# Two projections' weights: split into two parts once, the parts kept in a DRAM scratch and fetched for the later segments

## The chip, the core and the metric

The kernel runs on one core of one Trainium2 chip. The metric is the device time of that core for one execution, in microseconds (us). The engines are named as the profile names them: PE is TensorE (PEld are its weight loads), DVE is VectorE, ACT is ScalarE, POOL is GpSimd and SP is SyncE, whose queue issues most of the transfers.

## The reference: what is computed

One layer of a streaming encoder for 1024 frames of a new stream and 64 frames of a running one, model width 1024, all in float32:

```python
h = _rms_norm(x, norm1_g)
parts = jnp.split(h @ w_in, np.cumsum(IN_SIZES)[:-1].tolist(), axis=-1)   # w_in: 1024 x 3080
o_a, s_new, conv_new = _gdn_mixer(...)      # gated delta rule, 4 heads, blocks of 64
o_b, v_rows = _gmlp_mixer(...)              # spatial gating over chunks of 128
o_c = _swa_prompt(...)  or  _swa_sample(...)   # sliding-window attention with sinks
x = x + jnp.concatenate([o_a, o_b, o_c], axis=-1) @ w_out                 # w_out: 1024 x 1024
h = _rms_norm(x, norm2_g)
x = x + (jax.nn.silu(h @ w_gate) * (h @ w_up)) @ w_down                   # 1024 x 2816 and back
```

## The kernel before

**Products in two parts.** A float32 operand is written as h + l: h is the value rounded to the matmul format `fp32r`, l the rest. A product is three matmuls (h·h, h·l, l·h). ACT makes h by a copy (`acopy`, line 86), DVE makes l by a subtraction (`tt`, line 92).

**Segments.** The 1088 frames go through the input projection in three segments (`SEGS`): frames 0 to 383, 384 to 767, and 768 to 1023 with the 64 sample frames. Each segment multiplies by the whole of `w_in`. The matrix is cut into 24 pieces of about 512 KB, in this order: two of `g0`, two of `sq`, twelve of the convolution channels (`p0`, `p1`), two of `u`, two of `vm`, four of `z`. The output projection takes `w_out` in four pieces per half of its columns; its first half of columns is used twice, for frames 0 to 767 (`wo_plan[0]`) and at the end for the rest (`wo_plan[2]`), its second half once (`wo_plan[1]`). So there are 84 pieces, 72 of them from `w_in`.

**The class `Weights`.** `load` starts the transfer of one raw piece into one of three buffers `wr` (line 120, SP's queue), always up to three pieces ahead. `split` turns the raw piece into its parts `hw` and `lw`: two ACT copies and two DVE subtractions (four each for the first two pieces). The parts lie in one of three slots of `wts`; a fourth slot (`he`, `le`) is there during the output projection alone. The matmuls read the parts. When the last one of a piece has read them, its slot goes to the piece three places later.

**What PE does meanwhile.** The matmuls of the projections (`mm<-xh,hw` and the like: 24 for a group, in a bank `mm`) alternate with short ones of the mixers (all `ax<-...`): the delta rule, the attention, the gating, which ACT and DVE feed. `g0`, `sq` and `vm` go by frames: a group takes both pieces of such a pair, 12 matmuls on the first and 12 on the second, so both stay in their slots for three groups. The others go by channels: one group to a piece.

**After the mixers.** `out_proj` handles the first six blocks of 128 frames, `out_last(1, ...)` and then `out_last(0, wo_plan[2], o)` the last three. While these run, DVE and ACT also prepare the feed-forward stage: sums and splits of the normalised input (`x<-x,x`, `x_sums`), the same for its first weights (`w<-w,w`, `w_sums`, `w_split`). When the last group of a block is done, DVE adds it to the residual (`last_y`), ACT and POOL compute the norm (`norm2`), PE transposes the result (line 275), and the feed-forward matmuls (line 1462) go on with it.

**The order of instructions** on each engine is set by a list scheduler when the program is built: it orders them by a cost model of its own, so an instruction removed on one engine can move others. On the chip each engine, and each queue, works through its own list in order. From the feed-forward stage's last weights on the order is written by hand.

Of the kernel before, what the change touches and what calls it, by code (L numbers as in the profile page):

```python
# [7 lines left out]
F32 = mybir.dt.float32  # L8
# [4 lines left out]
ALU = mybir.AluOpType  # L13
# [40 lines left out]
def hybrid_step(ctx, tc, x_prompt, x_sample, cache_k, cache_v, st_gdn, st_conv, norm1_g, w_in, conv_w, a_log,  # L54
# [3 lines left out]
    V, A, G, T, SP = nc.vector, nc.scalar, nc.gpsimd, nc.tensor, nc.sync  # L58
# [17 lines left out]
    def sb(p, shape, tag, dt=F32, bufs=None):  # L76
        return p.tile(shape, dt, tag=tag, name=tag, bufs=bufs)
# [7 lines left out]
    def acopy(out, in_, scale=1.0):  # L85
        return A.activation(out=out, in_=in_, func=AF.Copy, scale=scale)  # L86
# [4 lines left out]
    def tt(out, in0, in1, op):  # L91
        return V.tensor_tensor(out=out, in0=in0, in1=in1, op=op)  # L92
# [8 lines left out]
    class Weights:  # L101
        def __init__(self):
            self.src, self.free, self.fresh, self.raw, self.got = [], [], [], {}, {}
            self.nd = self.ns = self.want = 0
            self.retired = None

        def slots(self, p, n, tag):
            self.free += [(p, f"{tag}{i}") for i in range(n)]

        def add(self, a, b, parts):  # L110
            self.src.append((a, b, parts))
            return len(self.src) - 1

        def load(self):
            i = self.nd
            a, b, parts = self.src[i]
            r = sb(wp, [128, 1056], "wr", bufs=3)
            v = r[:, :a * b].rearrange("p (a b) -> p a b", a=a)
            for lo, hi, k0, k1, c0, c1, s in parts:
                SP.dma_start(out=v[lo:hi, k0:k1, c0:c1], in_=s)  # L120
            self.raw[i] = r
            self.nd += 1

        def split(self):
            i = self.ns
            while self.nd <= i:
                self.load()
            a, b, _ = self.src[i]
            r, n = self.raw.pop(i), a * b
            p, t = self.free.pop(0)  # L130
            h = sb(p, [128, 1056], "h" + t, F32R)
            l = sb(p, [128, 1056], "l" + t, F32R)
            m = b if i < 2 else n // 2
            for c in range(0, n, m):
                acopy(h[:, c:c + m], r[:, c:c + m])
                tt(l[:, c:c + m], r[:, c:c + m], h[:, c:c + m].bitcast(F32), ALU.subtract)
            self.got[i] = ((p, t), h[:, :n].rearrange("p (a b) -> p a b", a=a),
                           l[:, :n].rearrange("p (a b) -> p a b", a=a))
            self.ns += 1
# [38 lines left out]
    W = Weights()  # L178
# [3 lines left out]
    plan = []  # L182
    for s in range(3):
        d = {}
# [17 lines left out]
    wo_plan = []  # L202
    for h in (0, 1, 0):
        c0 = 512 * h
        ids = []
        for kk in range(3):
            s_ = w_out[0, kk * 256:kk * 256 + 256, c0:c0 + 512].rearrange("(k p) c -> p k c", p=128)
            ids.append(W.add(2, 512, [(0, 128, 0, 2, 0, 512, s_)]))
        s_ = []
        for kv in range(2):  # L210
            s_.append((64 * kv, 64 * kv + 64, 0, 2, 0, 512,
                       w_out[0, 768 + 128 * kv:896 + 128 * kv, c0:c0 + 512].rearrange("(g d) c -> d g c", d=64)))
        ids.append(W.add(2, 512, s_))
        wo_plan.append(ids)

    wg_ = w_gate[0].rearrange("(k p) c -> p k c", p=128)
    wu_ = w_up[0].rearrange("(k p) c -> p k c", p=128)
# [1118 lines left out]
    def x_sums(c):  # L1336
        R = raw[c]
        B11, B21, B12, B22 = R[0, 0], R[1, 0], R[0, 1], R[1, 1]

        def split(n, v, late=0):  # L1340
            h, lo = x_tile(c, late=late > 0), x_tile(c, late=late > 1)
            acopy(h, v)
            tt(lo, v, h.bitcast(F32), ALU.subtract)
            X[c][n] = (h, lo)

        T1 = x_tile(c, F32)
        tt(T1, B12, B11, ALU.subtract)
        split("B11", B11)
        yield
        T2 = x_tile(c, F32)  # L1350
        tt(T2, B22, T1, ALU.subtract)
        split("T1", T1)
        yield
        T4 = x_tile(c, F32)
        tt(T4, B21, T2, ALU.subtract)
        split("T2", T2)
        yield
        split("B21", B21)
        yield
        tt(B12, B22, B12, ALU.subtract)  # L1360
        split("T3", B12, 1)
        yield
        split("B22", B22, 1)
        yield
        split("T4", T4, 2)
# [86 lines left out]
    later = []  # L1452
# [202 lines left out]
    def d_ops(kp):  # L1655
# [34 lines left out]
        def sub(n):  # L1690
# [11 lines left out]
            for j in range(2):  # L1702
# [3 lines left out]
                (("d", 0, diff, ("T1", "T2", "T3", "T4")), ("v", 0, lambda n: diff(n, V), ("T1", "T2", "T3", "T4")), ("r", 1, rnd, ("R1", "R2", "T13", "T24")),  # L1706
                 ("s", 1, sub, ("R1", "R2", "T13", "T24"))) for n in ns} | {
                     "L1": (1, lambda: load(0)), "L2": (1, lambda: load(1))}

    ORDER0 = ((-6, "aL1 aL2"), (0, "bL1 bL2 aT1d"), (1, "aT3d aR1r"), (2, "aT2d aR1s"), (3, "aT4d aT13r"),  # L1710
# [122 lines left out]
    for b, p, n, f in work:  # L1833
        k = b if p == "s" else (b, p, n)
# [23 lines left out]
    for u in range(22):  # L1858
# [6 lines left out]
        for i, s in enumerate(steps):  # L1865
# [7 lines left out]
            if i >= 7 or u not in (0, 21):  # L1873
                n = i - 7 if u in (0, 21) else i // 2
# [85 lines left out]
```

## Time and profile before

| | |
|---|---|
| median of 3 runs | 1357.01 us (1356.85 to 1358.77) |
| the profiled execution's own time | 1357.18 us |
| its span, first to last instruction | 1355.2 us |
| first segment, second, third (by the first `g0` matmul) | from 14.2, 168.8 and 341.8 us |
| output projection | 497.6 to about 621 us |
| feed-forward stage, gate and up | about 621 to 1085 us |
| feed-forward stage, down | to the end |

The profile shows one execution. Its page lists busy times, groups of instructions by line and tile, and the transfers; the trace behind it gives each instruction's start and duration, and what ended an engine's idle time. In a row of the timeline stand start, duration, engine, line, operation, tiles (out<-in), shape and count, and in brackets the idle time before it and who ended it. Matmuls overlap, so the time that one takes is the distance to the next start. A table of windows gives busy time and number of instructions for each engine in each stretch, then the granted clock of PE (1.00 is full), the busy share of the 16 DMA engines and their rate.

### The profile page before, as it was taken

The page shows a single profiled execution, that of the slowest core. Times are in us where ns is not written, and L with a number is a line of the kernel's source. Part 1 is how long each engine was busy: PE and PEld are TensorE (multiplying, and loading weights), DVE is VectorE, ACT ScalarE, POOL GpSimd, SP SyncE. Part 2 cuts the span into 40 slices and gives each one's busy share as a digit, 9 for nine tenths or more (in the row PEclk, how much of TensorE's full clock was granted, in tenths as well). Part 3 has the DMA queues.
Part 4 walks back from the last instruction along what each step waited for, and adds up shares of the span by engine and source line. Part 5 has one row for each costly group of instructions (what it writes and reads, how often), then busy time and mean ns, then how long its engine had stood idle before and what let it go on. Part 6 is the DMA issues. An engine that isn't in the chain of part 4 may idle for free.

```text
span 1355.2 us, 26537 instructions
## 1 busy us (share of the span) xinstructions
PE 1316.4 (97%) x9922; PEld 1170.9 (86%) x9922; DVE 986.2 (73%) x2286; ACT 683.4 (50%) x1725; POOL 183.4 (14%) x250
## 2 busy tenths in 40 slices
PE   6999999999999999998999999999999988999997
PEld 6988888888878887787999999999999976777784
DVE  6887877867788785588866777667776687767764
ACT  7677376674667653556555554455544532222202
POOL 3100130101121210100000000000000343232104
PEclk9999999999999999998999999999999999999999
DMA  8422342223233161322434544355443499666645
GB/s 259 122 79 64 82 116 78 79 64 80 70 93 94 49 214 51 121 78 86 126 120 152 176 136 124 111 156 175 132 124 112 159 320 335 223 225 238 215 142 198
DMA packets 205011, 189.00 MB, mean 139 GB/s; under 512 B 13931, under 2 KB 174160, under 8 KB 204882
## 3 DMA queue, kind: packets, MB, share of 16 engines
q1 hardware_dynamic: 196690, 174.71, 41.8%
q10 hardware_dynamic: 6704, 8.36, 1.7%
q0 software_dynamic: 1488, 4.23, 0.9%
q8 instruction: 78, 1.28, 0.4%
q14 instruction: 51, 0.42, 0.1%
HBM read 135.72 MB, written 51.61 MB: 138 GB/s over the span
## 4 chain that ended last, share of the span: by engine, by line
PE 83%; issue 6%; DVE 5%; ACT 2%; DMA 2%; POOL 1%; POOLq 0%; SPq 0%; ACTq 0%; DVEq 0%
PE ax L1462 29%; PE mm L95 26%; PE ax L95 11%; PE ax L1775 8%; PE mm L1462 5%; DVE x L92 2%; PE mm L1775 1%; PE ax L503 1%; PE ax L275 1%; DVE lw L92 1%; POOL x L1789 1%; PE ax L838 1%; DMA hd<-w 1%; DMA xs<-in_x_prompt_dram 0%; DVE tr L89 0%
## 5 line engine op out<-in xcount | busy, mean ns | idle before, releaser
L1462 PE MATMUL ax<-x,w 128*128 128x256 f32 (+1 forms) x2552 | 358.6, 287 | 0.0
L1462 PEld LDWEIGHTS ax<-x,w 128*128 128x128 f32 x2552 | 334.2, 190 | 0.3 <-ACT x L86 0.2
L92 DVE TENSOR_TENSOR w<-w,w 128x512 fp32r<-128x512 f32 (+1 forms) x242 | 164.6, 689 | 85.0 <-PE ax L1462 54.1
L95 PE MATMUL mm<-xh,hw 128*128 128x384 f32 (+1 forms) x432 | 151.3, 350 | 0.0
L95 PE MATMUL mm<-xl,hw 128*128 128x384 f32 (+1 forms) x432 | 143.5, 332 | 0.0
L95 PE MATMUL mm<-xh,lw 128*128 128x384 f32 (+1 forms) x432 | 143.1, 331 | 0.0
L92 DVE TENSOR_TENSOR x<-ax,x 128x512 f32<-128x512 f32 (+1 forms) x144 | 98.4, 687 | 58.2 <-PE ax L1775 47.7
L1775 PE MATMUL ax<-x,w 128*128 128x512 f32 x480 | 130.9, 397 | 9.6 <-DVE x L92 9.6
L86 ACT ACTIVATE hw<-wr 128x512 fp32r<-128x512 f32 (+2 forms) x168 | 99.7, 619 | 65.6 <-PE mm L95 55.0
L92 DVE TENSOR_TENSOR lw<-wr,hw 128x512 fp32r<-128x512 f32 (+2 forms) x168 | 110.8, 674 | 25.0 <-ACT hw L86 24.3
L1775 PEld LDWEIGHTS ax<-x,w 128*128 128x128 f32 x480 | 90.3, 190 | 33.1 <-DVE x L92 13.6
L1462 PE MATMUL ax<-xr,w 128*128 128x288 f32 x616 | 116.0, 296 | 1.2 <-DVE s L92 1.2
L86 ACT ACTIVATE w<-w 128x512 fp32r<-128x512 f32 x154 | 94.8, 624 | 31.4 <-PE mm L1462 14.4
L1462 PEld LDWEIGHTS ax<-xr,w 128*128 128x128 f32 x616 | 94.9, 188 | 1.5 <-DVE s L92 1.5
L95 PEld LDWEIGHTS mm<-xh,hw 128*128 128x128 f32 x432 | 81.1, 188 | 10.1 <-issue 7.3
L86 ACT ACTIVATE s<-ax 128x256 f32<-128x256 f32 (+1 forms) x132 | 51.9, 394 | 74.1 <-PE ax L1462 73.7
L95 PEld LDWEIGHTS mm<-xl,hw 128*128 128x128 f32 x432 | 81.4, 189 | 1.3 <-issue 0.7
L95 PEld LDWEIGHTS mm<-xh,lw 128*128 128x128 f32 x432 | 81.1, 188 | 1.2 <-issue 0.3
L1775 PE MATMUL ax<-f,w 128*128 128x512 f32 x220 | 72.5, 399 | 2.8 <-ACT w L86 1.6
L1678 POOL TENSOR_TENSOR w<-x 128x512 f32<-128x512 f32 x6 | 8.9, 1490 | 488.7 <-PE ax L1462 442.1
L1462 PE MATMUL mm<-x,w 128*128 128x256 f32 (+1 forms) x528 | 70.6, 289 | 0.0
L89 DVE SCALAR_TENSOR_TENSOR tr<-tr,cw 128x384 f32<-128x384 f32 (+1 forms) x108 | 64.1, 594 | 7.2 <-ACT tr L86 6.2
(360 smaller groups left out, 2551.0 us busy)
## 6 DMA issues: line engine op xcount, KB each, us to landing
wr<-in_w_in_dram SPq DMA_DIRECT2D x72, 512.0 KB, 3.9
hd<-e SPq DMA_DIRECT2D x140, 256.0 KB, 2.3
w<-hd SPq DMA_DIRECT2D x140, 256.0 KB, 4.6
w<-in_ffn_w_gate_dram SPq DMA_DIRECT2D x44, 256.0 KB, 3.5
w<-in_ffn_w_up_dram SPq DMA_DIRECT2D x44, 256.0 KB, 3.4
x<-in_ffn_w_down_dram SPq DMA_DIRECT2D x12, 512.0 KB, 3.7
wr<-in_w_out_dram SPq DMA_DIRECT2D x9, 512.0 KB, 4.4
y<-in_x_prompt_dram SPq DMA_DIRECT2D x8, 512.0 KB, 7.7
```

Source lines behind the costliest of these rows:

```text
L86: return A.activation(out=out, in_=in_, func=AF.Copy, scale=scale)
L89: return V.scalar_tensor_tensor(out=out, in0=in0, scalar=s, in1=in1, op0=op0, op1=op1)
L92: return V.tensor_tensor(out=out, in0=in0, in1=in1, op=op)
L95: return T.matmul(out, lhsT, rhs, start=start, stop=stop)
L275: T.transpose(b[k // 4][:, (k % 4) * r:(k % 4) * r + r], x[:r, k * 128:k * 128 + 128], ident[:r, :r])
L503: T.transpose(b[u // 4][:, (u % 4) * 128:(u % 4) * 128 + 128], src(u).rearrange("p h i -> p (h i)"), ident)
L838: T.transpose(PTp[0:r0 + cnt, j, kv, :], P[:, kv, 128 * j:128 * j + r0 + cnt], ident)
L1462: T.matmul(ps[:, :NB[c]], a[:, k, :], b[:, k, :], start=first and i == 0, stop=i == 11, skip_group_check=not first)
L1678: eng.tensor_tensor(out=block(t), in0=a, in1=b, op=ALU.subtract)
L1775: T.matmul(ps, l, r, start=fresh and m == 0, stop=m == 3 * len(kps) - 1, skip_group_check=not fresh)
L1789: G.tensor_tensor(out=yf[t][:, c], in0=block(slot), in1=yf[t][:, c], op=ALU.add)
```

## The change

For some pieces both parts are written to a DRAM tile (`wk`, two planes of 128 x 1056) right after the split, on SP's queue. A later piece with the same content is not loaded raw and not split: at the place in the program where `split` stood, two transfers on SP's queue fetch h and l from the scratch straight into the slot.

- The 20 pieces `p0`, `p1`, `u`, `vm`, `z` of the first segment are written, and fetched for the second and the third.
- The 4 pieces `g0`, `sq` are split in the first and again in the second segment, written there, and fetched for the third.
- The 4 pieces of `wo_plan[0]` are written, and fetched for `wo_plan[2]`.

So 28 pieces are written (56 transfers of about 512 KB), 48 are fetched (96 such transfers), and 48 raw loads (512 KB each) with 48 splits go. The fetch into a slot waits until PE has read the slot's former piece, and all fetches stand in one queue, in the order of the pieces. Arithmetic and results are the same.

```diff
+            self.kept, self.again = {}, {}
...
+        def keep(self, i, *later):
+            self.kept[i] = tc.dram_tile([2, 128, 1056], F32, name="wk%d" % i)
+            for j in later:
+                self.again[j] = self.kept[i]
+
         def load(self):
             i = self.nd
+            if i in self.again:
+                self.nd += 1
+                return
...
-            r, n = self.raw.pop(i), a * b
+            n = a * b
             p, t = self.free.pop(0)
             h = sb(p, [128, 1056], "h" + t, F32R)
             l = sb(p, [128, 1056], "l" + t, F32R)
-            m = b if i < 2 else n // 2
-            for c in range(0, n, m):
-                acopy(h[:, c:c + m], r[:, c:c + m])
-                tt(l[:, c:c + m], r[:, c:c + m], h[:, c:c + m].bitcast(F32), ALU.subtract)
+            if i in self.again:
+                for j, x in enumerate((h, l)):
+                    SP.dma_start(out=x[:, :n].bitcast(F32), in_=self.again[i][j, :, :n])
+            else:
+                r = self.raw.pop(i)
+                m = b if i < 2 else n // 2
+                for c in range(0, n, m):
+                    acopy(h[:, c:c + m], r[:, c:c + m])
+                    tt(l[:, c:c + m], r[:, c:c + m], h[:, c:c + m].bitcast(F32), ALU.subtract)
+                if i in self.kept:
+                    for j, x in enumerate((h, l)):
+                        SP.dma_start(out=self.kept[i][j, :, :n], in_=x[:, :n].bitcast(F32))
...
+    def pieces(d):
+        return d["g0"] + d["sq"], [i for g in range(2) for _, _, i in d["p%d" % g]] + d["u"] + d["vm"] + d["z"]
+
+    parts = [pieces(d) for d in plan]
+    for i, j in zip(parts[1][0], parts[2][0]):
+        W.keep(i, j)
+    for i, j, k in zip(*[q[1] for q in parts]):
+        W.keep(i, j, k)
+    for i, j in zip(wo_plan[0], wo_plan[2]):
+        W.keep(i, j)
```

**What moves, first place: DVE at the end of the output projection.** `lw_8120` is the l part of the last piece of `wo_plan[2]`; the `w` and `x` rows belong to the feed-forward stage; `y_7077` before, `y_6981` now, is the first addition of `last_y`. Before:

```order
L92 TENSOR_TENSOR w_8116<-w_8049,w_8115 128x512
L92 TENSOR_TENSOR x_8112<-x_8063,x_8111 128x1024
L92 TENSOR_TENSOR lw_8120<-wr,hw_8119 128x512 x2
L92 TENSOR_TENSOR w_8132<-w_8043,w_8131 128x512
L92 TENSOR_TENSOR w_8136<-w_8071,w_8135 128x512
L92 TENSOR_TENSOR w_8146<-w_8045,w_8145 128x512
L92 TENSOR_TENSOR w_8424<-w_8301,w_8303 128x512
L92 TENSOR_TENSOR y_7077<-mm,y_7077 128x512
```

Now:

```order
L92 TENSOR_TENSOR w_8007<-w_7940,w_8006 128x512
L92 TENSOR_TENSOR x_8003<-x_7954,x_8002 128x1024
L92 TENSOR_TENSOR w_8021<-w_7934,w_8020 128x512
L92 TENSOR_TENSOR w_8025<-w_7962,w_8024 128x512
L92 TENSOR_TENSOR w_8035<-w_7936,w_8034 128x512
L92 TENSOR_TENSOR y_6981<-mm,y_6981 128x512
L92 TENSOR_TENSOR y_6982<-mm,y_6982 128x512
```

The subtractions of the split are gone (the earlier ones of this stretch too), and one sum for the second weight block now stands behind `last_y`'s additions instead of ahead of the first.

**Second place: PE in the third segment, where `g0` ends and `sq` begins.** `hw_4714`, `hw_4932` are the h parts of the two `sq` pieces before; now they are `hw_4696` and `hw_4910`. Before:

```order
L95 MATMUL mm<-hw_4714,xl 128x256
L95 MATMUL mm<-hw_4932,xh 128x256
L95 MATMUL mm<-lw_4933,xh 128x256
L95 MATMUL mm<-hw_4932,xl 128x256
L95 MATMUL mm<-hw_4932,xh 128x256
```

Now:

```order
L95 MATMUL mm<-hw_4696,xl 128x256
L95 MATMUL mm<-hw_4910,xh 128x256
L95 MATMUL ax<-w,Z 64x128 x4
L95 MATMUL mm<-hw_4696,xh 128x256
L95 MATMUL mm<-lw_4697,xh 128x256
L95 MATMUL mm<-hw_4696,xl 128x256
L95 MATMUL mm<-hw_4696,xh 128x256
L95 MATMUL mm<-lw_4697,xh 128x256
L95 MATMUL mm<-hw_4696,xl 128x256
L95 MATMUL mm<-hw_4696,xh 128x256
L95 MATMUL mm<-lw_4697,xh 128x256
L95 MATMUL mm<-lw_4911,xh 128x256
```

After one matmul on the second piece's h part, four short ones and eight of the next group are drawn forward; then the second piece's l part is needed.

**Third place: PE in the second segment,** where the attention's weights are transposed (`ax<-cst,P`) between matmuls of a group. Before:

```order
L95 MATMUL ax<-w,Z 64x128 x2
L95 MATMUL mm<-xh,hw_3084 128x384
L838 MATMUL ax<-cst,P 128x128
L95 MATMUL mm<-xl,hw_3084 128x384
L838 MATMUL ax<-cst,P 128x128 x3
L95 MATMUL mm<-xh,lw_3085 128x384
```

Now:

```order
L95 MATMUL ax<-w,Z 64x128 x2
L866 MATMUL ax<-cst,P 128x128 x4
L95 MATMUL mm<-xh,hw_3132 128x384
L95 MATMUL mm<-xl,hw_3132 128x384
L95 MATMUL mm<-xh,lw_3133 128x384
```

Short matmuls stand together here and at some other places of the second and third segment. In the first segment PE's order is unchanged.

## The prediction

> **What bounds the kernel now.** I read the table of windows first: busy time and count on PE, PEld, DVE, ACT and POOL, then granted clock, transfer share and GB/s.
>
> ```profile
> 25.00:175.00 150.00, 149.85 (x1415) 133.62 (x1415) 118.64 (x327) 95.47 (x277) 19.38 (x36) 1.00 0.37 101
> 175.00:335.00 160.00, 159.98 (x1485) 137.53 (x1484) 122.47 (x365) 102.66 (x303) 24.85 (x41) 1.00 0.29 77
> 335.00:490.00 155.00, 154.23 (x1483) 130.87 (x1483) 123.59 (x398) 98.31 (x314) 33.64 (x64) 1.00 0.29 79
> 490.00:585.00 95.00, 94.98 (x579) 72.25 (x579) 53.18 (x122) 48.46 (x106) 10.53 (x19) 1.00 0.38 131
> 600.00:612.00 12.00, 12.00 (x53) 9.34 (x51) 12.00 (x17) 7.57 (x11) 0.00 (x0) 1.00 0.05 13
> 612.00:616.00 4.00, 0.65 (x2) 0.50 (x2) 4.00 (x6) 0.98 (x1) 0.00 (x0) 0.83 0.61 166
> 616.00:622.00 6.00, 6.00 (x20) 4.83 (x19) 4.78 (x8) 2.05 (x3) 0.74 (x2) 0.55 0.70 243
> ```
>
> From 25 to 585 us, where 76 of the 84 pieces are split, PE stands still for under 1 us in all. A busy PE may hide short waits, so I also read what PE waited for from 25 to 640 us:
>
> ```profile
> PE mm L95 <- DVE lw L92: 3.3, 1, 3.3
> ```
>
> A split ends one PE wait only, and it lies between the output projection and the feed-forward stage. There the timeline shows what is late:
>
> ```profile
> 611.21 0.62 PE L95 MATMUL mm<-hw,oh 128*128 128x512 f32 x2
> 614.67 1.29 DVE L92 TENSOR_TENSOR lw<-wr,hw 128x512 fp32r<-128x512 f32 x2
> 615.42 0.79 PE L95 MATMUL mm<-lw,oh 128*128 128x512 f32 x1 [3.35 <-DVE lw L92]
> 618.29 0.69 DVE L92 TENSOR_TENSOR y<-mm,y 128x512 f32<-128x512 f32 x1
> 629.29 0.71 PE L275 MATMUL ax<-cst,wr 64*128 64x64 f32 x8 [1.34 <-ACT wr L86]
> ```
>
> DVE is busy throughout (12.00 of 12, 4.00 of 4) and reaches the last `lw` at 614.67. PE idles 3.35 us for it and then runs at a clock of 0.55. The residual's `y` comes at 618.29, and eleven microseconds later, when the third block's norm has gone through ACT and POOL, PE makes the last transposes at 629.29 and is dense from there on.
>
> **The change part by part.**
>
> *Splits removed:* 48 pieces, two halves each.
>
> ```profile
> L86 ACT ACTIVATE hw<-wr 128x512 fp32r<-128x512 f32 (+2 forms) x168 | 99.7, 619 | 65.6 <-PE mm L95 55.0
> L92 DVE TENSOR_TENSOR lw<-wr,hw 128x512 fp32r<-128x512 f32 (+2 forms) x168 | 110.8, 674 | 25.0 <-ACT hw L86 24.3
> ```
>
> 96 x 619 ns = 59.4 us of ACT and 96 x 674 ns = 64.7 us of DVE. For 44 of the 48 pieces PE's own matmuls cover them (159.98 of 160 us, 154.23 of 155), so I cost them at nothing. The other four are those of `wo_plan[2]`.
>
> *The end of the output projection: -4.2 us.* DVE's groups from 592 to 618.3 us, with busy time and mean:
>
> ```profile
> L92 DVE TENSOR_TENSOR x<-x,x 128x1024 fp32r<-128x1024 f32 (+1 forms) x11 | 13.2, 1219 | 0.4 <-ACT x L86 0.4
> L92 DVE TENSOR_TENSOR w<-w,w 128x512 fp32r<-128x512 f32 (+1 forms) x12 | 7.7, 684 | 0.0
> L92 DVE TENSOR_TENSOR lw<-wr,hw 128x512 fp32r<-128x512 f32 x6 | 3.9, 686 | 0.0
> ...
> 595.26 0.64 ACT L86 ACTIVATE w<-w 128x512 fp32r<-128x512 f32 x1 [1.42 <-DMA w<-in_ffn_w_gate_dram]
> ```
>
> DVE idles 0.4 us in 26. The six `lw` of the row took 3.9 us of busy time, the pair at 614.67 1.29; consecutive ones overlap a little, so I estimate that the six gone are worth 3.6 us, and the `w` sum that moves behind `y` another 0.6. Not all of it arrives: in ACT's new list the rounding of the second `x` tile stands behind a copy that waits for the gate weights (landed by 595.26), and DVE waits for that rounding. Laying the new lists of DVE and ACT out with these durations, that costs 1.0. So `y` starts at 618.29 - 4.2 + 1.0 = 615.1. PE isn't in its way: at 611.7 it has 14 matmuls left, at 12/53 = 0.23 us each, and without the wait it is through at 614.9. From `y` to the last transposes the same layout gives 10.0 us instead of 11.0, because ACT now takes the first two blocks' sums of squares back to back. 625.1 against 629.29 is 4.2 us. Bounds: 5.5 if DVE never waits (3.6 + 0.6 + 1.0, rounded up), 1.9 if only the last pair of `lw` and the sum count.
>
> *The fetch that comes late: +0.6 us.* A slot has to be read out before its fetch starts. Where `g0` gives way to `sq` in the third segment:
>
> ```profile
> 352.15 0.28 PE L95 MATMUL mm<-lw,xh 128*128 128x264 f32 x1
> 355.91 0.28 PE L95 MATMUL mm<-hw,xh 128*128 128x256 f32 x1
> x<-in_ffn_w_down_dram SPq DMA_DIRECT2D x12, 512.0 KB, 3.7
> y<-in_x_prompt_dram SPq DMA_DIRECT2D x8, 512.0 KB, 7.7
> ```
>
> The slot is free at 352.15 + 0.28 = 352.43, the piece that follows is read from 355.91: 3.5 us. The nearest row is the 512 KB load in rows of 4 KB, 3.7 us to landing; h is some 0.3 late with the queue's wake-up. The l part follows by 512 KB at 243/0.70 = 347 GB/s, 1.5 us, while the eight matmuls drawn forward and the four short ones ask for it 1.6 us after h. I take 0.6, between 0 and 4.2 (with 7.7 us, the row of nine loads queued at once). What queues behind it on SP are only later fetches. [...]
>
> *The other fetches: 0.* The piece three places later gets the slot:
>
> ```profile
> 201.27 0.34 PE L95 MATMUL mm<-xh,lw 128*128 128x384 f32 x1
> 215.19 0.45 PE L95 MATMUL mm<-xh,hw 128*128 128x384 f32 x1
> ```
>
> That is most pieces; the shortest in the projection is the second `vm` piece:
>
> ```profile
> 448.62 0.30 PE L95 MATMUL mm<-xh,lw 128*128 128x320 f32 x1
> 457.33 0.28 PE L95 MATMUL mm<-hw,xh 128*128 128x256 f32 x1
> ```
>
> 13.6 us there, 8.4 here, against 3.7 + 1.5 = 5.2 for both parts. The last piece of `wo_plan[2]` has 7 (estimated from the order of the matmuls; PE wants its h at 611.21).
>
> *Stores: 0.* 40 stores of 512 KB in the first window add 140 GB/s to 101, in a share of 0.37; 243 GB/s took 0.70. On SP they wait for the same `lw` for which the raw load behind them waits anyway.
>
> *PE's order: -1.0 us.* Counted in the two lists, the second and third segment have 203 changes between `mm` and `ax` instead of 239: 18 insertions fewer. An ordinary one:
>
> ```profile
> 204.16 0.34 PE L95 MATMUL mm<-xh,lw 128*128 128x384 f32 x1
> 204.43 0.44 PE L95 MATMUL ax<-w,Z 64*64 64x128 f32 x4
> 204.79 0.44 PE L95 MATMUL mm<-xh,hw 128*128 128x384 f32 x1
> 205.07 0.34 PE L95 MATMUL mm<-xl,hw 128*128 128x384 f32 x1
> 205.25 0.34 PE L95 MATMUL mm<-xh,lw 128*128 128x384 f32 x1
> ```
>
> And one of the kind that mostly goes:
>
> ```profile
> 221.65 0.34 PE L95 MATMUL mm<-xh,lw 128*128 128x384 f32 x1
> 221.83 0.27 PE L838 MATMUL ax<-cst,P 128*128 128x128 f32 x1
> 221.85 0.42 PE L95 MATMUL mm<-xh,hw 128*128 128x384 f32 x1
> 222.12 0.49 PE L838 MATMUL ax<-cst,P 128*128 128x128 f32 x3
> 222.36 0.42 PE L95 MATMUL mm<-xl,hw 128*128 128x384 f32 x1
> 222.62 0.33 PE L95 MATMUL mm<-xh,lw 128*128 128x384 f32 x1
> ```
>
> A matmul of a group takes 0.18 us (205.07 to the next at 205.25). The first insertion lasts 0.91 from 204.16 to 205.07; two matmuls and the four short ones (0.36) make 0.72, so it costs 0.2. The second lasts 0.97 for three matmuls and four short ones: hardly 0.05 over. 18 of these give 3.6 at most and, if the merged ones wait longer, a loss of 1; I take 1.0, nearer to the second.
>
> *Sum:* 1357.18 (the profiled execution) - 4.2 + 0.6 - 1.0 = 1352.6. The median lies 0.2 lower: **1352.4 us**.
>
> **The rivals.**
>
> *A, more is freed than I count* (every insertion at 0.2, DVE never waits, no late fetch): 1357.0 - 3.6 - 5.5 = 1347.9. For it: the mixers' chains run through ACT and DVE, which lose 60 us of work. Against: PE stands still for under 1 us in all of these 560. Taken halfway, anything below 1351.
>
> *B, the wait only changes its name.* Gate weights and fetches share one queue, the fourth gate load now behind a fetch that waits for PE; if ACT's roundings slip by it, the end of the projection gains 1.9 or nothing: 1354.7 to 1356.6. For it: ACT already waits 1.42 us for these weights. Against: the fourth is wanted only by the seventh copy.
>
> *C, slower: fetches land after their need.* The raw loads ran three pieces ahead into buffers of their own; a fetch can't start before its slot is read out. If both parts took 12 us instead of 5.2, `sq` would stall 6.6, and the pieces with 8.4 to 11.3 us of lead, about six, some 13 together: 1352 + 19 = 1371. It turns the sum from about 9.5 us on. For it: 7.7 us for one queued load. Against: a share of 0.29 in these windows. [...]
>
> **How the numbers follow.** Forecast (1351 to 1354.3) 0.5, A 0.15, B 0.25, C 0.1. No change means within 0.2%, 2.7 us, about what such runs can tell: B above 1354.3 is that, so faster 0.65, same 0.25, slower 0.1. The likeliest is 1352.4. The range 1348.5 to 1357.0 leaves out C, A's far end and B's: about 0.2.
>
> **What would show it.** In the changed profile no `lw` ends a PE wait near 615 us and no clock below 0.9 stands there; the `y` addition and the last transposes come 3 to 4 us earlier, counted from the first transposes of that stage; a short PE wait for a fetched `hw` or `lw` appears near 356 us, and nowhere else in the segments; the windows of the second and third segment have the same PE count in a length shorter by up to 1 us each, with about 60 us less on ACT and on DVE. I am wrong if PE's waits name fetched parts several times, if the gate weights end DVE's or ACT's waits before `y`, or if a segment is shorter by more than 2 us.

## The result, and the profile after

The changed kernel takes 1349.68 us, median of 4 runs (1349.1 to 1352.28), beside 1357.22 us for the kernel before (4 runs): a ratio of 0.9945, 95% interval 0.9929 to 0.9961, or 7.5 us less. Forecast were 1352.4 us, in a range of 1348.5 to 1357.0. The profiled execution took 1349.63 us, with a span of 1347.9 us.

Three marks on PE divide the span: the first matmul of the output projection, the last transposes of the norm behind it, and the first matmul of the second half of the feed-forward stage. Of the kernel before (the second mark, 629.29, stands in the prediction):

```profile
497.58 0.50 PE L95 MATMUL mm<-hw,oh 128*128 128x512 f32 x1
...
1095.72 1.09 PE L1775 MATMUL ax<-x,w 128*128 128x512 f32 x4
```

Of the changed kernel:

```profile
494.53 0.50 PE L95 MATMUL mm<-hw,oh 128*128 128x512 f32 x1
...
621.41 0.71 PE L303 MATMUL ax<-cst,wr 64*128 64x64 f32 x8 [1.67 <-ACT wr L86]
...
1087.84 1.08 PE L1803 MATMUL ax<-x,w 128*128 128x512 f32 x4
```

| stretch | before | changed | difference |
|---|---|---|---|
| to the first out-projection matmul | 497.58 | 494.53 | -3.05 |
| from it to the last transposes | 131.71 | 126.88 | -4.83 |
| from them to the second half of the feed-forward stage | 466.43 | 466.43 | 0 |
| from there to the end of the span | 259.5 | 260.1 | +0.6 |

The first segment is as long as before, the second (by the first `g0` matmuls, 168.79 and 341.03 us now) is 0.79 us shorter, the third, up to the first mark, 2.28. The windows of the changed kernel, shifted to about the same work (columns as in the prediction):

```profile
25.00:175.00 150.00, 149.85 (x1416) 133.62 (x1415) 118.57 (x327) 95.51 (x276) 19.39 (x36) 1.00 0.77 255
175.00:334.20 159.20, 158.72 (x1478) 137.29 (x1479) 99.33 (x320) 80.58 (x259) 21.14 (x41) 1.00 0.46 155
334.20:487.00 152.80, 151.00 (x1499) 129.79 (x1496) 102.48 (x357) 76.86 (x270) 28.99 (x65) 1.00 0.51 173
...
612.00:616.00 4.00, 1.66 (x15) 1.45 (x14) 2.02 (x4) 3.26 (x6) 2.31 (x4) 1.00 0.98 377
```

PE is still full in the segments, though now it stands still for 0.5 and 1.8 us in the second and third instead of 0.0 and 0.8. The rate in the first window rises from 101 to 255 GB/s with the stores, and PE's 149.85 does not move. Around 614 us the clock stays at 1.00. The groups of the splits, 168 instructions each before:

```profile
L92 DVE TENSOR_TENSOR lw<-wr,hw 128x512 fp32r<-128x512 f32 (+2 forms) x72 | 46.0, 657 | 12.9 <-ACT hw L86 11.0 <-DMA wr<-in_w_in_dram 1.4
...
L86 ACT ACTIVATE hw<-wr 128x512 fp32r<-128x512 f32 (+2 forms) x72 | 41.8, 606 | 26.0 <-PE mm L95 24.1 <-issue 1.9
```

64.8 us less on DVE, 57.9 less on ACT. What PE waited for from 25 to 500 us:

```profile
PE ax L95 <- DVE tr L484: 1.0, 1, 1.0
PE ax L95 <- DVE PT L871: 0.4, 2, 0.2
PE ax L866 <- ACT P L86: 0.4, 1, 0.4
PE ax L95 <- DVE w L89: 0.3, 1, 0.3
```

No fetched part is among them, and no `lw` behind them. Four small waits of the mixers, 2.1 us together, stand where there were 0.7.

### The profile page after: what moved, and what is told of

The parts are those of the page before. It is cut to its first block, busy times and chain, and to the rows that moved or that the text cites. A ratio compares the mean times of both kernels' runs of the same rounds, so it can differ in the third digit from the quotient of the medians.

```text
span 1347.9 us, 26489 instructions
## 1 busy us (share of the span) xinstructions
PE 1311.6 (97%) x9922; PEld 1169.9 (87%) x9922; DVE 936.8 (70%) x2190; ACT 635.4 (47%) x1629; POOL 175.3 (13%) x250
## 4 chain that ended last, share of the span: by engine, by line
PE 82%; DVE 6%; issue 6%; POOL 2%; DMA 2%; ACT 2%; POOLq 0%; ACTq 0%; DVEq 0%
PE ax L1490 29%; PE mm L95 25%; PE ax L95 11%; PE ax L1803 8%; PE mm L1490 5%; DVE x L92 2%; PE mm L1803 1%; DMA hd<-w 1%; PE ax L303 1%; PE ax L531 1%; DVE tr L89 1%; POOL x L1817 1%; PE ax L866 1%; POOL ssk L288 1%; DMA xs<-in_x_prompt_dram 0%
## 5 line engine op out<-in xcount | busy, mean ns | idle before, releaser
L1490 PEld LDWEIGHTS mm<-x,w 128*128 128x128 f32 x528 | 67.9, 190 | 0.2 <-issue 0.2
L95 PE MATMUL mm<-hw,xh 128*128 128x256 f32 (+1 forms) x216 | 62.6, 294 | 0.0
```

What stands on the lines that cost most here:

```text
L95: return T.matmul(out, lhsT, rhs, start=start, stop=stop)
L1490: T.matmul(ps[:, :NB[c]], a[:, k, :], b[:, k, :], start=first and i == 0, stop=i == 11, skip_group_check=not first)
```

## The experiments

Two theories stood against each other for the first 3.05 us. "Order": PE's list has 18 insertions of short matmuls fewer, and each costs time. "Relief": ACT and DVE are less busy, and PE gains whatever its order. For the 4.83 us the question was whether the four pieces of `wo_plan[2]` alone bring them. All runs, with the three marks' stretches of their profiles and the time against the kernel before on the same chip:

| run | to first out-projection matmul | to last transposes | last stretch | median us | ratio (95%) |
|---|---|---|---|---|---|
| `e1_old_order` | 499.00 | 126.86 | 259.5 | 1353.57 | 0.9966 (0.9954 to 0.9978) |
| `e2_new_order` | 500.46 | 131.68 | 261.4 | 1363.26 | 1.0041 (1.0029 to 1.0054) |
| `e3_wo_only` | 497.64 | 126.88 | 258.5 | 1352.88 | 0.9959 (0.9947 to 0.9971) |
| `e4_win_only` | 494.38 | 131.74 | 261.3 | 1355.19 | 0.9978 (0.9968 to 0.9987) |
| `e5_stores_only` | 497.68 | 131.78 | 263.9 | 1357.14 | 0.9996 (0.9987 to 1.0005) |
| `e6_fetch_x1` | 495.44 | 126.89 | 262.6 | 1353.39 | 0.9961 (0.9945 to 0.9977) |
| `e6_fetch_x2` | 495.59 | 126.88 | 261.1 | 1351.91 | 0.9963 (0.9952 to 0.9974) |
| `e7_more_changes` | 501.54 | 128.07 | 260.0 | 1358.07 | 1.0007 (0.9997 to 1.0016) |
| `e8_fewer_changes` | 492.68 | 126.89 | 260.9 | 1348.54 | 0.9927 (0.9915 to 0.9940) |
| `e9_fewer_more` | 495.07 | 126.98 | 260.8 | 1351.28 | 0.9953 (0.9940 to 0.9965) |
| `e10_changed_again` | 494.39 | 126.88 | 260.2 | 1349.78 | 0.9942 (0.9929 to 0.9956) |

The columns of stretches carry the readings, because the times also hold the last stretch. With the same work in it, it differs by several microseconds from profile to profile, and the times of one kernel alone spread as far: the twelve runs of `e5_stores_only` go from 1354.90 to 1361.68 us, and its profile is of the slowest. The stretch between the last transposes and the second half of the feed-forward stage isn't in the table: it is 466.4 to 466.5 us in every profile but two, 467.9 in `e3_wo_only` and `e6_fetch_x1` (the last section comes back to them).

**PE's order alone, both ways.** In `e1_old_order` and `e2_new_order` PE's list is fixed by order-only edges along a table (runs of positions in the order of the code):

```diff
+    traced = [i for i in nc.cur_bb.bb.instructions if i.engine == mybir.EngineType.PE and "Matm" in type(i).__name__]
+    want = [traced[a + k] for a, n in PE_ORDER for k in range(n)]
+    for p, i in zip(want, want[1:]):
+        tc.add_manual_dep(i, p.name, mybir.DependencyInfo(mybir.DependencyClass.NoSync, ...), reason="PE order")
```

> The changed kernel, with PE's matmuls up to the out-projection put back into the order of the kernel before (a table of positions, laid on the scheduler as order-only edges); fetches, stores and the missing splits stay. Theory 'order' (the 3.05 us that the stretch up to the first out-projection matmul gained come from 18 changes fewer between mm and ax): that matmul comes at 497.5 again (494.53 in the changed kernel, 497.58 before), the stretch from it to the last norm transposes stays at 126.9, the time is 1349.7 + 3.0 = 1352.7. Theory 'relief' (PE waits less on ACT and DVE, whatever its order): the matmul stays within 0.5 of 494.5, the time is 1349.7 to 1350.2.

The fetches without the new order bring the input projection nothing: 499.00, 1.4 us later than the kernel before. So "relief" falls. That it is later, "order" had not said; the timeline of this run shows most of the reason:

```profile
352.69 0.32 SPq L144 DMA_DIRECT2D hw<-wk  x1
353.10 0.38 SPq L144 DMA_DIRECT2D lw<-wk  x1
...
356.29 0.39 PE L95 MATMUL mm<-hw,xh 128*128 128x256 f32 x1
357.52 0.39 PE L95 MATMUL mm<-lw,xh 128*128 128x256 f32 x1 [0.85 <-DMA lw<-wk]
```

This is the late fetch of the prediction: h just in time, l 4.4 us after its issue. In the old order PE asks for l right behind h. This wait is 0.85 of the 1.4 us; the small waits of the mixers, 1.8 us in this run instead of 0.7, account for the rest.

> The kernel before, all splits in place, with PE's matmuls up to the out-projection in the order of the changed kernel. Theory 'order': first out-projection matmul at 494.6, the stretch behind it 131.7 as before, the time is 1357.2 - 3.0 = 1354.2. Theory 'relief': the new order has no worth by itself while ACT and DVE still split; the matmul comes at 497.6 or later, since work drawn forward waits for its inputs; 1357.2 to 1359.

Here "order" in its plain form falls: the new order on the kernel before makes it slower, by 2.9 us at the first mark and by 5.4 in all (in the profile, the last stretch is 1.9 us longer). Its waits of PE from 25 to 500 us:

```profile
PE ax L95 <- ACT tr L86: 2.6, 5, 0.9
PE ax L838 <- ACT P L86: 1.8, 2, 1.5
PE ax L95 <- DVE xv L92: 1.0, 1, 1.0
PE ax L95 <- DVE S L89: 0.4, 1, 0.4
PE ax L838 <- POOL tail L457: 0.3, 1, 0.3
```

They sum to 6.1 us. Without them this run would stand at 494.4, and the kernel before, without its 0.7, at 496.9: by this estimate the order saves 2.5 us of PE's own time, but it asks for results of ACT and DVE earlier, and with the splits in their lists PE waits 5.4 us longer for them. The changed kernel without its 2.1 us of waits would stand at 492.4, another 2.0 us lower; what they are stays open. Neither half gains alone. The scheduler finds the new order wherever the input projection's splits are replaced by fetches (`e4_win_only`), and keeps the old one where they stay (`e3_wo_only`, `e5_stores_only`): up to the first mark, 294 changes between `mm` and `ax` in the one trace, 330 in the two others.

**One projection at a time.** `e3_wo_only` drops the two loops of `W.keep` for the input projection, `e4_win_only` the one for the output projection.

> Only the four pieces of the output projection are kept and fetched again; the input projection splits all its 72 pieces as before. Theory 'end' (the splits of the last four pieces held up DVE and with it PE at the end of the projection): the stretch from the first out-projection matmul to the last norm transposes is 126.9 instead of 131.7, the first matmul stays at 497.5, the time is 1357.2 - 4.8 = 1352.4. Rival (the relief of the queue and of the raw buffers in the input projection has a part in it): 129 or more, 1354.5 or more.

> Only the pieces of the input projection are kept and fetched; the output projection splits all its twelve pieces. Theories 'end' and 'order': first out-projection matmul at 494.5, the stretch behind it 131.7 with a PE wait of about 3.3 us for the last lw, the time is 1357.2 - 3.0 = 1354.2. Rival: with the input projection's share gone the end also shortens, below 130, time below 1352.5.

Both come out as "end" and "order" say: 126.88 with PE's first mark at 497.64, and 494.38 with a stretch of 131.74. PE's waits from 25 to 640 us that a split ends, in the run without the output projection's pieces kept (none in the other):

```profile
PE mm L95 <- DVE lw L92: 3.3, 1, 3.3
```

By the ratios the two parts are worth 5.6 and 3.0 us (0.41% and 0.22% of 1357), together 8.6 beside 7.5 for both; the stretches say 4.8 and 3.2.

**The stores alone.** `keep` fills no `again`, so every piece is split as before and 28 are stored.

```diff
             self.kept[i] = tc.dram_tile([2, 128, 1056], F32, name="wk%d" % i)
-            for j in later:
-                self.again[j] = self.kept[i]
```

> The 56 stores of the parts stay, nothing is fetched: all 84 pieces are loaded raw and split as before, and PE's order is that of the kernel before. Theory 'stores cost nothing': first out-projection matmul at 497.6 and the stretch behind it 131.7, both within 0.3; the time is that of the kernel before. Rival (20 MB of stores in the first segment crowd the loads there, or a raw load waits behind a store on the queue): the second segment begins 1 us or more after 168.8, the time rises by as much.

The two stretches up to the last transposes are 0.1 us longer each than in the kernel before: no cost of the stores shows.

**More to fetch.** Behind the two fetches of a piece, one or two more of the same 512 KB into raw buffers that nobody reads; PE's order as in the changed kernel.

```diff
                 for j, x in enumerate((h, l)):
                     SP.dma_start(out=x[:, :n].bitcast(F32), in_=self.again[i][j, :, :n])
+                for j in range(2):
+                    SP.dma_start(out=sb(wp, [128, 1056], "wr", bufs=3)[:, :n], in_=self.again[i][j, :, :n])
```

> The changed kernel in its own order on PE, with one more transfer of 512 KB (the h part once more, into an unused raw buffer) on the same queue for each of the 48 fetched pieces, so 1.5 MB instead of 1 MB a piece. Theory 'fetches have room' (a piece has 6.3 us or more in the third segment, 1 MB takes about 3 us of it): the same time as the changed kernel, within 1 us. Rival 'at the edge' (the fetches just make it, as the h part at 354.5 does): waits of PE for fetched parts at several places, first out-projection matmul 4 us or more after 494.5.

> As the run before, with both parts fetched a second time into unused raw buffers: 2 MB a piece. At 347 GB/s, the rate that the prediction took from the busiest window, that is 6.0 us a piece, where a piece lasts 6.3 in the third segment. Theory 'fetches have room': the waits begin here, but stay small, first out-projection matmul 0 to 6 us after 494.5. Rival 'at the edge': 12 us or more.

The windows from 195 to 340 and from 340 to 490 us, with two more:

```profile
195.00:340.00 145.00, 143.80 (x1352) 123.24 (x1351) 91.14 (x284) 66.72 (x218) 15.52 (x29) 1.00 0.86 313
340.00:490.00 150.00, 148.19 (x1450) 127.56 (x1449) 101.39 (x355) 76.52 (x268) 29.05 (x65) 1.00 0.82 294
```

In the changed kernel the same windows move 156 and 178 GB/s. At 2.0 and 1.65 times these rates one fetch comes late, by 1.0 us at 196.4 us, where the second segment turns to its first fetched piece; with one more it is the same place and 1.1 us. (The median of `e6_fetch_x1` is 3.7 us above the changed kernel's instead of 1: in its profile 0.9 lie ahead of the first mark, the others in the two stretches behind the last transposes, where no fetch of parts is left.) The extra transfers wait for no slot. In `e6_fetch_x2` ten of them were issued from 165 to 191 us, ahead of most parts, and from 203 to 265 us each one or more right behind a pair; so they load the queue but seldom stand between a slot and its fetch. How much later a fetch could start was not tried. "At the edge" falls for the rate.

**The price of an insertion.** In `e7_more_changes` the first matmul of a group's next run stands in the middle of the short ones ahead of it, at 32 places (rows of the order, before and now, as a sketch):

```
mm ... mm | ax ax ax ax | mm mm ...
mm ... mm | ax ax | mm | ax ax | mm ...
```

> The changed kernel with 32 changes of each direction between mm and ax more on PE in the second and third segment: at 32 places the first matmul of a group's next run is moved into the middle of the run of short matmuls ahead of it. No instruction more, no input later. Theory 'order' (each insertion costs 0.17, as 3.05 us for 18 say): 5.4 us more, first out-projection matmul at 500, time 1355.1. Rival (an insertion as such costs next to nothing, the gain came from where the short matmuls stand against their inputs): under 2 us more.

The first mark comes at 501.54, 7.0 us later. In the trace 27 of the 32 lie ahead of it (348 changes between `mm` and `ax` instead of 294) and five in the output projection, whose stretch grows by 1.19. That makes 0.26 us each ahead of the mark and 0.24 behind it, where the expectations below take 0.22 from 7.0 by 32. No new wait of PE came; two of the old ones are left, 0.6 us of 2.1:

```profile
PE ax L866 <- ACT P L86: 0.4, 1, 0.4
PE ax L95 <- DVE tr L484: 0.2, 1, 0.2
```

So an insertion costs time, as "order" says, and 0.17 was set too low. But 0.26 is a mean and not the price of each. Of the 18 that the changed kernel lost, by the traces before and after (where the other parts of the three segments differ by 0.05 us or less):

| part of the input projection | changes between `mm` and `ax` | changes of the tile's shape | length, us |
|---|---|---|---|
| second segment, `p0` to `u` | 78, now 62 | 82, now 79 | 98.13, now 98.05 |
| second segment, `z` | 22, now 20 | 36, now 33 | 35.72, now 34.99 |
| third segment, `g0` and `sq` | 16, now 12 | 21, now 19 | 24.80, now 24.22 |
| third segment, `p0` to `vm` | 84, now 70 | 98, now 87 | 101.61, now 99.92 |

Eight insertions went in the first row, seven of them beside the attention's transposes, and brought 0.08 us, while 0.5 us of waits appeared there. The other ten brought 3.0. The third column counts something else: how often a matmul's tile (`128*128`, `64*64` and so on in its row) differs from the one ahead of it. With the new waits added back, 0.5 us in the first row and 1.0 in the last, the four parts gained 0.6, 0.7, 0.6 and 2.7 us, which is 0.2 to 0.3 us for each such change (0.21 for the 40 that `e7_more_changes` adds, up to the first mark). In the trace of the kernel before, from 25 us to the first mark, a matmul of a group is followed by the next after 0.17 us (median, waits left out), by a short one of its own shape `128*128` after 0.18 and by one of `64*64` after 0.27. So it may be the change of shape that costs, and not the change from `mm` to `ax`; no run here parts the two.

**Fewer changes.** `e8_fewer_changes` goes the other way from the changed kernel at 18 places, `e9_fewer_more` at 27; `e10_changed_again` is the changed kernel beside them.

> The changed kernel with 18 insertions fewer (six in the first segment, twelve in the second and third): at 18 places one to eight matmuls of a group stand ahead of the short matmuls that they parted from the next short ones, so two runs of short matmuls become one. At a price of 0.22 us each (7.0 us for 32 in the run with more changes): 4.0 us less, first out-projection matmul at 490.5 instead of 494.5, 1345.7 where the changed kernel has 1349.7. Rival (the short matmuls that come up to 1.4 us later hold up a chain of ACT and DVE, and PE waits for it): 493 or more.

> As the run before, at nine more places, where the two runs belong to the same block's inversion and are closer to depending on one another: 27 insertions fewer. By the price alone 5.9 us less, first out-projection matmul at 488.6, 1343.8. Rival: waits of PE on ACT and DVE eat the nine (each short matmul of these chains is followed by an ACT copy or a DVE operation of 0.3 us or more that the next one needs): no earlier than the run with 18.

> The changed kernel unaltered, beside the two runs with fewer changes: 1349.7, first out-projection matmul at 494.5, the stretch behind it 126.9. Only the stage change to the second half of the feed-forward stage, where PE's half clock fell for 3.4 to 10.2 us in the profiles so far, should differ, by up to 1.5 us.

PE's waits that the changed kernel does not have, with 18 and then with 27:

```profile
PE ax L95 <- ACT tr L86: 1.1, 3, 0.5
PE ax L95 <- DVE Z L611: 0.4, 2, 0.2
```

```profile
PE ax L95 <- DVE Z L611: 2.6, 6, 0.8
PE ax L95 <- ACT tr L86: 2.2, 3, 1.1
```

With 18 fewer the first mark comes 1.7 us earlier than beside it in `e10_changed_again`, against 4.0 by the price: the waits named take 1.5 of the rest, and the six of the first segment brought only 0.4. The time is 1348.54 beside 1349.78, but the intervals overlap. With 27 fewer the waits, 4.8 us, cost more than was saved. These two attempts brought 1.7 us at most; other ways of merging were not tried. (The expectation of `e10_changed_again` overlooks `e3_wo_only`, where the granted clock was 1.00 from 1090 to 1144 us.)

## Why the prediction was right, and where it was not

The direction and the range held; the gain was 7.5 us, not 4.6, so the time missed the stretch from 1351 to 1354.3 that had been given half of the chances. It lies below 1351, where the prediction had rival A begin, and A's three conditions are what happened: insertions near their full price, no wait of DVE, no late fetch. By name the forecast's terms were the right ones; A had the better sizes.

Of its signs, the clock stayed at 1.00 near 615 us and no `lw` ended a wait there, but no PE wait for a fetched part came near 356 us. Two signs of being wrong appeared. The third segment is shorter by 2.28 us, which is the term of PE's order below. And gate weights ended two of ACT's waits before `y`:

```profile
590.39 0.63 ACT L86 ACTIVATE w<-w 128x512 fp32r<-128x512 f32 x1 [6.95 <-DMA w<-in_ffn_w_gate_dram]
...
595.51 0.63 ACT L86 ACTIVATE w<-w 128x512 fp32r<-128x512 f32 x1 [0.99 <-DMA w<-in_ffn_w_gate_dram]
```

These cost DVE nothing, as the term of the projection's end shows.

*Splits hidden behind PE's own matmuls: right.* 44 of the 48 pieces cost PE nothing before, and in the old order taking them away gained nothing (`e1_old_order`).

*The end of the output projection, -4.2: measured -4.83, right in cause.* `e3_wo_only` gives the whole of it. Its two parts were off by 1.2 us one way and 0.6 the other, so some of the closeness is luck. DVE's groups from 592 to 612 us in the changed kernel:

```profile
L92 DVE TENSOR_TENSOR x<-x,x 128x1024 fp32r<-128x1024 f32 (+1 forms) x9 | 10.7, 1217 | 0.0
L92 DVE TENSOR_TENSOR w<-w,w 128x512 fp32r<-128x512 f32 (+1 forms) x11 | 7.2, 680 | 0.0
```

The 1.0 us that DVE was to wait for ACT's rounding behind the gate weights did not come: DVE had other work in hand (idle 0.0). So `y` gained 4.4 instead of 3.2, counted from the first mark: 618.29 - 497.58 = 120.71 before, and now 610.84 - 494.53 = 116.31. The chain behind it:

```profile
610.84 1.28 DVE L92 TENSOR_TENSOR y<-mm,y 128x512 f32<-128x512 f32 x2
...
611.56 1.06 ACT L293 ACTIVATE xt<-y 128x1024 bf16<-128x1024 f32 x1 [4.22 <-DVE y L92]
...
612.62 1.04 ACT L293 ACTIVATE xt<-y 128x1024 bf16<-128x1024 f32 x1
612.80 0.70 POOL L287 TENSOR_SCALAR ss<-ss 128x1 f32<-128x1 f32 x1 [32.77 <-ACT xt L293]
...
613.58 0.88 POOL L288 TENSOR_TENSOR ss<-ss,mhalf 128x1 f32<-128x1 f32 x1
614.49 1.15 ACT L86 ACTIVATE wr<-y,ss 128x1024 f32<-128x1024 f32 x1 [0.74 <-POOL ss L288]
...
615.69 1.09 PE L303 MATMUL ax<-cst,wr 128*128 128x128 f32 x8 [2.35 <-ACT wr L86]
```

The two sums of squares stand back to back, as forecast. But POOL's two small steps took 0.70 and 0.88 us; the second block's, in the same trace, took 0.19 and 0.55, as did those of the first two blocks in the kernel before. So from `y` to the last transposes 0.43 was gained, not 1.0. PE now waits 2.35 us for the norm where it waited 3.35 for a split: rival B's new name for the wait, at 0.7 of its length and with a granted clock of 1.00 from 616 to 622 us instead of 0.55. In `e1_old_order` PE's rows behind the same wait of 2.35 us are slower (last section), and its stretch is the same, 126.86.

*The late fetch, +0.6: measured 0 in the changed kernel, 0.85 in the old order.* The place was right: in the old order this fetch is late. The step that failed is the time of h:

```profile
350.66 0.28 PE L95 MATMUL mm<-hw,xh 128*128 128x264 f32 x1
350.97 0.32 SPq L144 DMA_DIRECT2D hw<-wk  x1
351.38 0.38 SPq L144 DMA_DIRECT2D lw<-wk  x1
...
354.54 0.33 PE L95 MATMUL mm<-hw,xh 128*128 128x256 f32 x1
...
356.33 0.40 PE L95 MATMUL mm<-lw,xh 128*128 128x256 f32 x2
```

I had h start when the l part of the former piece was read out and take the 3.7 us of another load. But h's tile is free when the former h part is read, at 350.94, 0.12 earlier; the fetch was issued 0.03 later and landed after 3.47 us, at 354.44, 0.1 before PE asked. So the 0.3 us by which h was to be late were not there, and for the other 0.3 of the term the prediction gave no row. Its comparison for l held: l would land at 355.8, an estimate by the 4.4 us of `e1_old_order`, and the eight matmuls drawn forward put off its use to about 356.4. In the old order they don't, and l is late. Over the whole trace the medians to landing are:

```profile
lw<-wk SPq DMA_DIRECT2D x46, 512.0 KB, 4.5
hw<-wk SPq DMA_DIRECT2D x46, 512.0 KB, 3.7
```

*The other fetches and the stores, 0: right* (`e6_fetch_x1`, `e6_fetch_x2`, `e5_stores_only`).

*PE's order, -1.0: measured -3.05; this is the term that was mis-sized.* Between an insertion priced at 0.2 and one at 0.05 I chose nearer to the second, since that kind mostly goes, and took about 0.06 for all 18. The step that failed is the one price for all. For its own kind the 0.05 was about right: from `p0` to `u` of the second segment, where seven of the eight that went are of it, 0.08 us were gained, or 0.6 without the 0.5 us of new waits, 0.07 each. The other ten brought 3.0 us, 0.3 each. By the mean of `e7_more_changes` 18 times 0.26 is 4.7, less about 1.4 for the small waits that the mixers gained (2.1 instead of 0.7): 3.3, near the 3.05 seen, but with prices so uneven that is partly chance. The two rows that it chose between differ in the tile: the 0.2 was at `64*64`, the 0.05 at `128*128`, the shape of the group's own matmuls. What the prediction did not see at all is the condition: the same order on lists that still hold the splits loses 2.9 us (`e2_new_order`).

*Not forecast: +0.6 in the last stretch*, within what one kernel's runs differ by. Of its start, 50 us before and then now have nearly the same work and another clock:

```profile
1098.00:1148.00 50.00, 41.23 (x170) 32.38 (x170) 38.45 (x59) 14.35 (x30) 16.34 (x13) 0.97 0.95 327
```

```profile
1090.00:1140.00 50.00, 43.17 (x168) 34.00 (x167) 38.19 (x58) 14.34 (x30) 16.08 (x13) 0.90 0.96 325
```

Rival C (fetches late) did not show: one fetch is on time by 0.1 us, the others have room.

## What to carry to other kernels

When the engine that bounds a stage is full, work taken from other engines may gain nothing by itself, as here; look at what the freed lists let a scheduler do with the bound engine's order. Price that order by a run that adds the cost (here 0.26 us per insertion in the mean), not by one place in the trace, and part by part: eight of the 18 insertions were worth next to nothing, the other ten 0.3 us each. Where a single wait of the bound engine hangs on a busy helper, count the helper's list up to that point: that term came within 15%, though two errors in it partly cancelled. Before trusting a difference of one or two microseconds, split the span at marks and see whether it lies in the stretch that was changed.

## What the runs showed of the hardware

Around and behind PE's wait of 3.35 us, which ends at 615.42, the granted clock of the kernel before was 0.83 from 612 to 616 us and 0.55 from 616 to 622. In the changed kernel PE's wait of 2.35 us ends at 615.69, and the clock was 1.00 in both windows. `e1_old_order` has a wait of the same length and slower rows behind it. The changed kernel:

```profile
615.69 1.09 PE L303 MATMUL ax<-cst,wr 128*128 128x128 f32 x8 [2.35 <-ACT wr L86]
617.21 1.09 PE L303 MATMUL ax<-cst,wr 128*128 128x128 f32 x8 [0.43 <-ACT wr L86]
618.06 1.68 PE L1490 MATMUL ax<-x,w 128*128 128x256 f32 x12
```

`e1_old_order`:

```profile
620.14 1.14 PE L303 MATMUL ax<-cst,wr 128*128 128x128 f32 x8 [2.35 <-ACT wr L86]
621.67 1.97 PE L303 MATMUL ax<-cst,wr 128*128 128x128 f32 x8 [0.38 <-ACT wr L86]
623.29 2.20 PE L1490 MATMUL ax<-x,w 128*128 128x256 f32 x12
```

So the length of this wait does not tell the two apart; what does, these runs do not show.

What the slower rows added to a stretch differed too. From the first mark to the last transposes `e1_old_order` took 126.86 us and the changed kernel 126.88; PE waits 3.1 and 4.4 us for the norm in that stretch. In `e3_wo_only` and `e6_fetch_x1` slower rows stand right behind the last transposes, where PE is dense. The changed kernel, then these two:

```profile
622.05 11.13 PE L1490 MATMUL ax<-x,w 128*128 128x256 f32 x86
```

```profile
625.16 8.00 PE L1490 MATMUL ax<-x,w 128*128 128x256 f32 x51
```

```profile
623.10 10.11 PE L1492 MATMUL ax<-x,w 128*128 128x256 f32 x69
```

That is 0.129 us a matmul in the changed kernel, 0.157 and 0.147 in the two. At 0.129 the 51 and 69 matmuls would take 6.6 and 8.9 us, 1.4 and 1.2 less (an estimate from these rows); the stretch that follows the last transposes is 1.5 us longer in both, 467.9.

The last stretch goes only partly with the mean granted clock of the profile. At 0.998 it took 258.5 us (`e3_wo_only`), at 0.992 it took 263.9 (`e5_stores_only`). But at 0.996 it took 259.5 in the kernel before and 260.1 in the changed one, at 0.997 it took 261.1 (`e6_fetch_x2`), and at 0.994 from 260.0 (`e7_more_changes`) to 261.4 (`e2_new_order`). What else moves it stays open.
